# Attention outputs with features on partitions, summed over three groups with weights spread by DMA

## The chip, the cores and the metric

One core of one Trainium2 chip runs the whole step. The metric is device microseconds of that core, as the median of several executions. Its engines are TensorE (PE, matmuls, with its weight loads shown apart as PEld), VectorE (DVE), ScalarE (ACT), GpSimd (POOL) and SyncE (SP), which here issues most of the DMA transfers. Each engine runs its own list of instructions in order; a wait on another engine holds up all that stands behind it in the same list.

## The reference, cut to what matters

The kernel is one step of a decoder for 1024 prompt tokens and 64 sample tokens of width 1024. It has a projection to queries, keys, values and gates, causal pooling as a second branch, dilated attention in three groups of four heads of 64 features, gates, an output projection and an MLP. The groups have reach and stride (128, 1), (512, 4) and (2048, 16). Over 1024 tokens the third group's keys of one residue all fit one block. Each group gives values and the log of its softmax sum, and the groups are mixed with a softmax over these:

```python
def masked_softmax_stats(s, valid):
    s = jnp.where(valid, s, -jnp.inf)
    m = jnp.max(s, axis=-1, keepdims=True)
    p = jnp.exp(s - m)
    den = jnp.sum(p, axis=-1, keepdims=True)
    return p / den, (m + jnp.log(den))[..., 0]

def combine_groups(outs, lses, dtype):
    wts = jax.nn.softmax(jnp.stack(lses, axis=0), axis=0)
    o = jnp.einsum('gbth,gbthd->bthd', wts, jnp.stack(outs, axis=0))
    B, T = o.shape[:2]
    return o.reshape(B, T, ATTN_OUT_WIDTH).astype(dtype)

    branch_b = jnp.einsum('btc,cd->btd', attn, w_pb)
```

## The kernel before

All large products are matmuls over operands that are split into two parts (a rounded one and the rest), with three products summed. Weights come by DMA in panels into one of three places and are split there by ACT (line 108) and DVE (line 109). The stretch from 60 to 166 us makes the third group's queries, keys and values (g2) and its attention, 166 to 300 the second's (g1), 300 to 396 the first's (g0); to 472 us come the gates and the end of the attention, then dense products to the end.

Prompt tokens are in eight blocks of 128 per group. A block's projection is a gemm over 24 matmuls for each of q, k and v (tiles pq, pk, pqk, pv). Between two gemms, and in the middle of each, the kernel calls `step()`, which lets every running generator go on to its next `yield`. So a `yield` in the attention's code is one place further in PE's list, about one gemm or half a gemm, and PE's list is the order of the program text. The order on DVE, ACT and POOL is set by a scheduler, not by the text; each engine then runs its list in order. `behind_pe` ties an instruction to the place of PE's list where it was written. `soon` puts it off to the next step.

For each block `attention()` (from line 574) makes the scores (tile sg, line 586, two halves of the rows), masks them (line 595, a DVE operation that also gives the statistics st), takes exponentials (line 596, ACT), transposes the probabilities on PE (tile tp, line 605), copies them out (pT, line 608), and multiplies them with the values (tile po, line 617): the transposed probabilities are the stationary operand, 128 columns, and the 64 features of a head move, so that the result has tokens on partitions and features along the row. With two key blocks there are 16 such products per block, with one there are 8. ACT copies the result to oc (line 620), and DVE puts the statistics beside it (line 621).

For g2 and g1 oc is stored in DRAM (o_d, lines 694 and 697). For g0 it stays; the other groups' oc of the same 128 tokens are loaded (olg0b, lines 687 and 688), the statistics are gathered (md, lines 700 and 701), `weights()` (lines 625 to 636) forms the softmax over the groups by eight small operations (last one line 635), and `weigh()` (lines 638 to 643) multiplies and adds on DVE. Three steps later (five for the last block) two transposes per block (tile tc, line 709) turn the sum to features on partitions, ACT copies it out (line 651), and it is stored to attn_d (line 656). `branches()` (from line 1009) loads it back as raw_b, with the pooling branch, and splits it into the operand ab of the product pb (and pa). The gate's products (pga, pgb) run meanwhile; line 998 on DVE and line 999 on ACT follow each.

The copies of the new keys for the cache are made in kw (line 917, two buffers) and stored.

## Time and profile before

| | |
|---|---|
| median of 3 runs | 1532.62 us (1532.09 to 1534.24) |
| the profiled execution's own time | 1536.69 us |
| its span | 1534.8 us |
| granted clock, mean | 0.997 |
| PE busy | 1519.1 us (99%) |
| DVE busy | 880.0 us (57%) |
| ACT busy | 519.1 us (34%) |
| POOL busy | 204.3 us (13%) |
| PE's share of the chain that ended last | 89% |

The page is of one execution. Busy time of an engine is the union of its instructions; a matmul's own duration holds a tail that overlaps the next one's, so the pace of a group of matmuls is read from its start to the start of what follows. Rows of groups give line, engine, operation, the tiles out<-in, shapes, count, busy time and mean ns of one, and the idle time ahead of them with what ended most of it. Rows in order of time give start, duration and the same names, with an idle time in brackets. The granted clock is a share of full speed.

### The profile page before, as it was taken

The page shows a single profiled execution, that of the slowest core. Times are in us where ns is not written, and L with a number is a line of the kernel's source. Part 1 is how long each engine was busy: PE and PEld are TensorE (multiplying, and loading weights), DVE is VectorE, ACT ScalarE, POOL GpSimd, SP SyncE. Part 2 cuts the span into 40 slices and gives each one's busy share as a digit, 9 for nine tenths or more (in the row PEclk, how much of TensorE's full clock was granted, in tenths as well). Part 3 has the DMA queues.
Part 4 walks back from the last instruction along what each step waited for, and adds up shares of the span by engine and source line. Part 5 has one row for each costly group of instructions (what it writes and reads, how often), then busy time and mean ns, then how long its engine had stood idle before and what let it go on. Part 6 is the DMA issues. An engine that isn't in the chain of part 4 may idle for free.

```text
span 1534.8 us, 25518 instructions
## 1 busy us (share of the span) xinstructions
PE 1519.1 (99%) x9785; PEld 1474.7 (96%) x9785; DVE 880.0 (57%) x1948; ACT 519.1 (34%) x1613; POOL 204.3 (13%) x245
## 2 busy tenths in 40 slices
PE   9999999999899999999999999999999999999998
PEld 8989888889899999999999999999999999999998
DVE  7655656678755434344575565555555556655556
ACT  8567755677753222222331111111111211112100
POOL 1611256256200000010000000000000000000000
PEclk9999999999999999999999999999999999999999
DMA  5312678655455353584131331322312223222102
GB/s 200 104 50 87 190 168 201 184 138 135 128 147 186 127 180 109 165 264 168 64 107 54 107 104 57 107 69 91 107 63 97 92 72 110 70 95 100 35 8 117
DMA packets 104535, 178.65 MB, mean 116 GB/s; under 512 B 16919, under 2 KB 69725, under 8 KB 103198
## 3 DMA queue, kind: packets, MB, share of 16 engines
q1 hardware_dynamic: 98302, 126.70, 27.4%
q0 software_dynamic: 6112, 50.33, 9.7%
q8 instruction: 77, 1.26, 0.3%
q14 instruction: 44, 0.36, 0.1%
HBM read 155.54 MB, written 65.10 MB: 144 GB/s over the span
## 4 chain that ended last, share of the span: by engine, by line
PE 89%; DMA 3%; DVE 3%; ACT 2%; POOL 1%; issue 1%; SPq 0%; DVEq 0%; ACTq 0%; POOLq 0%
PE py L147 25%; PE pz L147 24%; PE pgb L147 6%; PE ph L147 6%; PE pqk L147 5%; PE pga L147 5%; PE pv L147 3%; PE pa L147 3%; PE a L261 3%; PE pb L147 2%; DMA raw_qkv<-in_w_in_dram 1%; PE pq L147 1%; PE pk L147 1%; PE pog1b L617 1%; DMA olg0b<-o_d 1%
## 5 line engine op out<-in xcount | busy, mean ns | idle before, releaser
L147 PE MATMUL pz<-act,places 128*128 128x384 f32 (+1 forms) x2304 | 382.4, 326 | 0.0
L147 PE MATMUL py<-z,places 128*128 128x384 f32 (+1 forms) x2304 | 381.5, 327 | 0.0
L147 PEld LDWEIGHTS pz<-act,places 128*128 128x128 f32 x2304 | 379.5, 188 | 0.4
L147 PEld LDWEIGHTS py<-z,places 128*128 128x128 f32 x2304 | 379.5, 188 | 0.0
L1194 DVE TENSOR_TENSOR y<-y,py 128x384 f32<-128x384 f32 (+1 forms) x360 | 188.2, 530 | 112.7 <-PE py L147 112.3
L1176 ACT ACTIVATE z<-r 128x384 fp32r<-128x384 f32 (+1 forms) x96 | 48.7, 508 | 323.9 <-DVE r L1175 323.9
L1175 DVE SCALAR_TENSOR_TENSOR r<-pz,rbh 128x384 f32<-128x384 f32 (+1 forms) x96 | 51.2, 534 | 173.2 <-PE pz L147 173.2
L1205 POOL DMA_DIRECT2D out_kv_sample_dram<-in_cache_kv_dram x44 | 21.8, 495 | 934.7 <-ACT places L108 913.1
L108 ACT ACTIVATE places<-raw_u 128x512 fp32r<-128x512 f32 x64 | 38.4, 627 | 266.7 <-PE py L147 259.9
L147 PE MATMUL pga<-act,places 128*128 128x384 f32 (+1 forms) x576 | 99.0, 330 | 0.0
L147 PE MATMUL pgb<-act,places 128*128 128x384 f32 (+1 forms) x576 | 97.8, 326 | 0.0
L147 PE MATMUL ph<-act,places 128*128 128x384 f32 (+1 forms) x576 | 95.9, 327 | 0.0
L147 PEld LDWEIGHTS pga<-act,places 128*128 128x128 f32 x576 | 95.6, 190 | 0.3
L147 PEld LDWEIGHTS pgb<-act,places 128*128 128x128 f32 x576 | 95.4, 188 | 0.0
L147 PEld LDWEIGHTS ph<-act,places 128*128 128x128 f32 x576 | 94.8, 188 | 0.3
L550 POOL TENSOR_TENSOR mr<-ms,mhalf 128x4 f32<-128x4 f32 (+2 forms) x39 | 51.3, 1317 | 109.1 <-DVE ms L549 103.9
L147 PE MATMUL pqk<-places,act 128*128 128x512 f32 x240 | 60.7, 402 | 0.0
L1178 DVE TENSOR_TENSOR z<-q,z 128x384 fp32r<-128x384 f32 (+1 forms) x96 | 51.3, 535 | 8.1
L109 DVE TENSOR_TENSOR places<-raw_d,places 128x512 fp32r<-128x512 f32 x64 | 41.4, 689 | 23.2 <-ACT places L108 23.2
L147 PEld LDWEIGHTS pqk<-places,act 128*128 128x128 f32 x240 | 44.5, 191 | 9.8 <-issue 0.2
L757 POOL TENSOR_TENSOR pcv<-pcv,sc 128x256 f32<-128x256 f32 x64 | 47.6, 772 | 42.6 <-DMA pcv<-in_cache_kv_dram 16.0
L1177 DVE TENSOR_TENSOR q<-r 128x384 f32<-128x384 f32 (+1 forms) x96 | 51.2, 535 | 2.7
(296 smaller groups left out, 2040.8 us busy)
## 6 DMA issues: line engine op xcount, KB each, us to landing
out_kv_sample_dram<-in_cache_kv_dram POOLq DMA_DIRECT2D x36, 960.0 KB, 5.6
raw_u<-in_w_up_dram SPq DMA_DIRECT2D x64, 256.0 KB
raw_d<-in_w_down_dram SPq DMA_DIRECT2D x64, 256.0 KB
raw_qkv<-in_w_in_dram SPq DMA_DIRECT2D x36, 256.0 KB
pck<-in_cache_kv_dram SPq DMA_DIRECT2D x32, 256.0 KB
pcv<-in_cache_kv_dram SPq DMA_DIRECT2D x32, 256.0 KB
out_kv_sample_dram<-in_cache_kv_dram POOLq DMA_DIRECT2D x8, 1008.0 KB, 5.4
kts<-in_kT_dram SPq DMA_DIRECT2D x20, 256.0 KB
```

Of the source, the lines that this page charges most:

```text
L108: ins = s_.activation(dst_hi, src, AF.Copy)
L109: v_.tensor_tensor(dst_lo, src, dst_hi.bitcast(F32), op=ALU.subtract)
L147: last_mm[0] = t_.matmul(out, lhs(a, k), rhs(b, k), start=(j == 0), stop=(j == len(terms) - 1))
L261: last_mm[0] = t_.matmul(pts[m][:, :n], wt[:, a, kk, m * P:(m + 1) * P], act4[b][kk][:, :, part4(c)], start=(p == 0 and kk == 0), stop=(p ...
L550: g_.tensor_tensor(r[:n, :H], ms[:n, :H], mhalf[:n, :H], op=ALU.pow)
L757: behind_pe(g_.tensor_tensor(tv, tv, sc[:, j + n, :].unsqueeze(2).to_broadcast([P, 4, HD]), op=ALU.mult))
L1175: v_.scalar_tensor_tensor(r[:, :n], pzs[m][:, :n], 0.0, rbh[:, c0:c0 + n], op0=ALU.max, op1=ALU.mult)
L1176: s_.activation(z[:, m, 0, :n], r[:, :n], AF.Square)
L1177: v_.tensor_tensor(q[:, :n], r[:, :n], r[:, :n], op=ALU.mult)
L1178: v_.tensor_tensor(z[:, m, 1, :n], q[:, :n], z[:, m, 0, :n].bitcast(F32), op=ALU.subtract)
L1194: v_.tensor_tensor(yc, yc, py[:, :n], op=ALU.add)
L1205: ins = g_.dma_start(d, a)
```

## The change

The product of probabilities and values is turned round: the values, 64 columns of a head, are the stationary operand and the transposed probabilities (128 tokens) move. The result has features on partitions, a head on the lower 64 and the next on the upper 64, so the array is used in two column halves; neighbouring products go to different halves. Their number is the same. Here are the products of one block of the third group on PE (tile po), with what follows them, before:

```order
L617 MATMUL pog2b_1547<-v_2_1068,pTg2b_0_1471 128x64 x2
L617 MATMUL pog2b_1547<-v_2_1068,pTg2b_1_1499 128x64 x2
L440 MATMUL pl_1_1555<-ext_429,lin 128x384
L570 MATMUL tqg2b_1559<-cst,qk_4_1336 128x128 x4
L147 MATMUL pv_5_1567<-places,act_74 128x256 x16
```

And the last two of the four after, with the same followers:

```order
L626 MATMUL pog2b_1546<-pTg2b_0_1471,v_2_1075 64x128
L626 MATMUL pog2b_1546<-pTg2b_1_1499,v_2_1075 64x128
L444 MATMUL pl_1_1553<-ext_434,lin 128x384
L579 MATMUL tqg2b_1557<-cst,qk_4_1339 128x128 x4
L147 MATMUL pv_5_1565<-places,act_74 128x256 x16
```

Before, two products of one half of the probabilities (pT ..._0) run, then two of the other (pT ..._1), each 128 partitions by 64. After, the output is 64 partitions by 128 and the halves alternate, twice pT ..._0 and pT ..._1.

Two blocks now share one tile oc of 512 columns. The results of g2 and g1 are stored by pairs in an order by features (o_d), the statistics stay in tiles (sta) and go through DRAM once per group (st_d) into md, which is there before g0 starts. g2's blocks are taken in another order (`res8`), with the same strides.

For g0 `weights()` lays its result out as 12 columns; one transpose per block (tile tw, line 751), one step behind `weights()`, gives 12 rows of 128; DVE copies them (wT, line 755), a pair's are stored (w_d, line 758), and `combine()` loads each row spread over 64 partitions (ww and w2) and the other groups' values (o1, o2), and multiplies and adds whole pairs (lines 695, 696, 697, 705 and 706). The transposes tc and the copies behind them are gone; attn_d is stored once per pair (line 708). PE around the weights of block 3, before, where the sum was transposed (tile tc, the operand oc is the finished sum):

```order
L147 MATMUL pv_7_5359<-places,nat_02_5165 128x256 x4
L147 MATMUL pv_7_5359<-places,nat_04_5167 128x256 x4
L147 MATMUL pv_7_5359<-places,nat_06_5169 128x256 x4
L709 MATMUL tcg0b_5389<-cst,ocg0b_5109 128x128 x2
L605 MATMUL tpg0b_0_5411<-cst,smg0b_0_5273 128x128 x4
L147 MATMUL pga_0_0_5448<-act_74,places 128x384 x8
```

And after (tile tw, the operand cw is the weights):

```order
L147 MATMUL pq_7_5135<-places,nat_02_5089 128x256 x4
L147 MATMUL pq_7_5135<-places,nat_04_5091 128x256 x4
L147 MATMUL pq_7_5135<-places,nat_06_5093 128x256 x4
L751 MATMUL twg0b_5173<-cst,cwg0b_5109 12x128
L615 MATMUL tpg0b_1_5176<-cst,smg0b_1_4966 128x128 x4
L596 MATMUL sg0b_0_5183<-qkTg0b_4796,qkTg0b_5036 128x128
```

The transpose of block 3 has moved from behind pv_7 to behind pq_7, two gemms earlier, and it waits for the weights rather than for the sum. DVE's list after, up to the copy behind that transpose (ce, cm and cw are the weights' tiles, ms_7_0 the mean squares of the queries of block 7, raw_ga a panel of the gates):

```order
L109 TENSOR_TENSOR places<-raw_ga_0_5341,places 128x512
L109 TENSOR_TENSOR places<-raw_ga_512_5345,places 128x512
L650 TENSOR_TENSOR cwg0b_5109<-ceg0b_5108,md 128x12
L809 TENSOR_TENSOR pcv_5047<-pcv_5047 128x512
L109 TENSOR_TENSOR places<-raw_ga_1024_5349,places 128x512
L558 TENSOR_SCALAR ms_7_0_5160<-ms_7_0_5160,xeps_68 128x4
L651 TENSOR_REDUCE cmg0b_5107<-cwg0b_5109 128x4
L810 TENSOR_TENSOR ss<-ss,pcv_5047 128x512
L652 RECIPROCAL cmg0b_5107<-cmg0b_5107 128x4
L654 TENSOR_TENSOR cwg0b_5109<-ceg0b_5108,cmg0b_5107 128x6x2
L913 TENSOR_REDUCE sfm<-osm 128x4
L755 COPY wTg0b_4942<-twg0b_5173 12x128
```

The weights of block 3 end in the row of line 654; three splits of raw_ga and the mean squares of block 7 stand ahead of it.

SP issues in `combine()` the loads of the spread weights and values. The line of kw now has one buffer, and the probabilities' pT two, not three. The diff, cut to its core:

```diff
     dp = pool("dram", space=DRAM)
-    o_d = [None, [dp.tile([512, 264], F32, name=f"o_d1_{h}") for h in range(2)], dp.tile([SEQ, 264], F32, name="o_d2")]
+
+
+    o_d = [None] + [dp.tile([P, 4, 2, R4 - 16], F32, name=f"o_d{g}") for g in (1, 2)]
+    st_d = [None] + [dp.tile([SEQ, 8], F32, name=f"st_d{g}") for g in (1, 2)]
+    w_d = [dp.tile([12, 2 * P], F32, name=f"w_d{u}") for u in range(4)]
...
-        st = rr(ap, [P, 8], F32, name=f"st{name}", tag="st", bufs=6)
+    def attention(g, b, keys, qT, name):
+
+
+        st = md[:, b, 0, :] if g == 0 else sta[g][:, res8(b), :]
...
-            pT = rr(ap, [P, 4, P], F32, name=f"pT{name}_{e}", tag="pT", bufs=3)
+            pT = rr(ap, [P, 4, P], F32, name=f"pT{name}_{e}", tag="pT", bufs=2)
             pTs.append(pT)
             s_.copy(pT[:, :2 * nk, :], tp[:, :2 * nk, :])
...
-        if ahead:
-            ahead()
-        po = short(f"po{name}")[:, :256]
-        for e in range(2):
-            for hp in range(2):
-                h = 2 * hp + e
-                for j, (_, vr) in enumerate(keys):
-                    t_.matmul(po[:, h * HD:(h + 1) * HD], pTs[e][:, hp * nk + j, :], vr[:, h * HD:(h + 1) * HD],
+        po = short(f"po{name}")[:, :256].rearrange("p (j t) -> p j t", j=2)
+
+        for hp in range(2):
+            for j, (_, vr) in enumerate(keys):
+                for e in range(2):
+                    h = 2 * hp + e
+                    t_.matmul(po[e * HD:(e + 1) * HD, hp, :], vr[:, h * HD:(h + 1) * HD], pTs[e][:, hp * nk + j, :],
                               start=(j == 0), stop=(j == nk - 1))
-        out = rr(ap, [P, 264], F32, name=f"oc{name}", tag="oc", bufs=2)
-        s_.copy(out[:, :256], po)
-        v_.tensor_copy(out[:, 256:], st)
-        return out
+        if b % 2 == 0:
+            pair[g] = rr(ap, [P, 512], F32, name=f"oc{name}", tag="oc", bufs=2)
+        dst = pair[g].rearrange("p (j t) -> p j t", j=2)
+        if g == 2:
+            s_.copy(dst[:, :, b % 2::2], po)
+        elif g == 1:
+            s_.copy(dst[:, :, b % 2 * P:(b % 2 + 1) * P], po)
+        else:
+            s_.copy(dst.rearrange("p j (q l) -> p j q l", q=4)[:, :, :, b % 2 * 32:(b % 2 + 1) * 32],
+                    po.rearrange("p j (l q) -> p j q l", q=4))
+
+    sta = [None] + [ap.tile([P, 8, 8], F32, name=f"sta{g}") for g in (1, 2)]
+    pair = {}
 
     def weights(nm, den, name):
 
         mm = rr(ap2, [P, 4], F32, name=f"cm{name}", tag="cm", bufs=2)
...
-        v_.tensor_reduce(mm, nm.rearrange("p g h -> p h g"), axis=AX.X, op=ALU.min)
+        behind_pe(v_.tensor_reduce(mm, nm.rearrange("p g h -> p h g"), axis=AX.X, op=ALU.min))
...
-        v_.tensor_tensor(e, e, mm.unsqueeze(1).to_broadcast([P, 3, 4]), op=ALU.mult)
-        return e
+        w = w.rearrange("p g h -> p (g h)")
+        v_.tensor_tensor(w.rearrange("p (x g y) -> p g y x", x=2, g=3), e.rearrange("p g (y x) -> p g y x", x=2),
+                         mm.rearrange("p (y x) -> p y x", x=2).unsqueeze(1).to_broadcast([P, 3, 2, 2]), op=ALU.mult)
+        return w
 
...
+    def combine(u, oc):
+        byq = lambda t: t.rearrange("p (j l q) -> p j q l", j=2, q=4)
+        tokens = slice(64 * u, 64 * u + 64)
+        def values(g, t):
+            dma(t.rearrange("p (x l) -> p x l", l=64), o_d[g][:, :, :, tokens].rearrange("p q j l -> p (q j) l"))
+            return t.rearrange("p (q j l) -> p j q l", q=4, j=2)
+        def scales(g, t):
+            for x in range(2):
+                behind_pe(dma(t[x * HD:(x + 1) * HD],
+                              bass.AP(tensor=w_d[u].tensor, offset=w_d[u].offset + (6 * x + 2 * g) * 2 * P,
+                                      ap=[[0, HD], [1, t.shape[1]]])))
+        acc = oc.rearrange("p (j q l) -> p j q l", j=2, q=4)
+        o1 = values(1, rr(ap2, [P, 512], F32, name=f"o1_{u}", tag="ow", bufs=1))
+        if u == 3:
+            o2 = values(2, rr(ap1, [P, 512], F32, name=f"o2_{u}", tag="qk", bufs=2))
+        yield
+        yield
+        ww = ap0.tile([P, 1024], F32, name=f"ww{u}", tag="smp")
+        scales(0, ww)
+        if u == 3:
+            w2 = rr(ap1, [P, 512], F32, name=f"w2_{u}", tag="qk", bufs=2)
+            scales(2, w2)
+        yield
+        yield
+        behind_pe(v_.tensor_tensor(acc, acc, byq(ww[:, :512]), op=ALU.mult))
+        v_.tensor_tensor(o1, o1, byq(ww[:, 512:]), op=ALU.mult)
+        v_.tensor_tensor(acc, acc, o1, op=ALU.add)
+        if u < 3:
+            yield
+            o2 = values(2, rr(ap2, [P, 512], F32, name=f"o2_{u}", tag="ow", bufs=1))
+            w2 = ww[:, :512]
+            scales(2, w2)
+            yield
+            yield
+        behind_pe(v_.tensor_tensor(o2, o2, byq(w2), op=ALU.mult))
+        v_.tensor_tensor(acc, acc, o2, op=ALU.add)
+        yield
+        behind_pe(dma_st(attn_d[:, :, :, tokens].rearrange("p j q l -> p (j q) l"), oc.rearrange("p (x l) -> p x l", l=64)))
...
-        oc = yield from attention(g, ([kept[g, b - 1]] if older else []) + [kept[g, b]], qkT, name,
-                                  None if g else others)
-        yield
-        if g == 2:
-            behind_pe(dma_st(o_d[2].rearrange("(l r) c -> r l c", r=8)[b], oc))
+        yield from attention(g, b, ([kept[g, b - 1]] if older else []) + [kept[g, b]], qkT, name)
+        oc = pair[g]
+        yield
+        if g:
+            if b % 2:
+                behind_pe(dma_st(o_d[g][:, b // 2].rearrange("p j l -> p (j l)"), oc))
+            if b == 7:
+                if g == 2:
+                    src, dst = sta[2].rearrange("p r c -> p (r c)"), st_d[2].rearrange("(l r) c -> l (r c)", r=8)
+                else:
+                    src, dst = sta[1].rearrange("p (x q) c -> p x (q c)", x=2), st_d[1].rearrange("(x l q) c -> l x (q c)", x=2, q=4)
+                behind_pe(dma_st(dst, src))
+                yield
+                yield
+                behind_pe(dma(md[:, :, g, :], st_d[g].rearrange("(b p) c -> p b c", p=P)))
+                done.add((g, "max"))
             return
-        if g == 1:
-            behind_pe(dma_st(o_d[1][b % 2].rearrange("(l r) c -> r l c", r=4)[b // 2], oc))
-            return
-        md = rr(ap2, [P, 3, 8], F32, name=f"md{name}", tag="md", bufs=2)
-        behind_pe(v_.tensor_copy(md[:, 0, :], oc[:, 256:]))
-        behind_pe(v_.tensor_copy(md[:, 1:, :], ol[:, :, 256:]))
-        e = weights(md[:, :, :4], md[:, :, 4:], name)
-        o3 = [x[:, :256].rearrange("p (h d) -> p h d", h=4) for x in (oc, ol[:, 0, :], ol[:, 1, :])]
-        weigh(o3, e)
-        for _ in range(5 if b == 7 else 3):
-            yield
-        tp = short4(f"tc{name}")
-        for j in range(2):
-            t_.transpose(tp[:, j, :], oc[:, j * P:(j + 1) * P], ident)
-        store_attn(tp[:, :2, :], P, t0, name)
+        assert {(1, "max"), (2, "max")} <= done
+        w = weights(md[:, b, :, :4], md[:, b, :, 4:], name)
+        yield
+        tp = short(f"tw{name}")[:12, :P]
+        t_.transpose(tp, w, ident)
+        if b % 2 == 0:
+            pair["w"] = rr(ap2, [12, 2 * P], F32, name=f"wT{name}", tag="wT", bufs=1)
+        wT = pair["w"]
+        v_.tensor_copy(wT[:, b % 2 * P:(b % 2 + 1) * P], tp)
+        if b % 2:
+            yield
+            behind_pe(dma_st(w_d[b // 2], wT))
+            yield from combine(b // 2, oc)
...
-            kw = rr(ap, [P, 256], F32, name=f"kw{g}_{b}", tag="kw", bufs=2)
+            kw = rr(ap, [P, 256], F32, name=f"kw{g}_{b}", tag="kw", bufs=1)
```

More of the change, by code (lines that the diff above doesn't have):

```diff
@@ L496, in block_cols, with res8 @@
             return act4[s][k][:, blk // 2, blk % 2 * P:(blk % 2 + 1) * P]
-        return act4[s][k][:, blk % 4, blk // 4:2 * P:2]
+        return act4[s][k][:, blk // 2, blk % 2:2 * P:2]
+    def res8(blk):
+        return blk // 2 + 4 * (blk % 2)
     nat = {}
@@ L573, in transposed @@
         v_.tensor_copy(dst[:, 2:, :n], tp[:, 2:, :n])
-    def attention(g, keys, qT, name, ahead=None):
-        st = rr(ap, [P, 8], F32, name=f"st{name}", tag="st", bufs=6)
+    def attention(g, b, keys, qT, name):
+        st = md[:, b, 0, :] if g == 0 else sta[g][:, res8(b), :]
         nk = len(keys)
@@ L643, in weigh @@
         v_.tensor_tensor(oc[0], oc[0], oc[2], op=ALU.add)
-    def store_attn(tp, n, t0, name):
-        w, h = n // 4, t0 // P % 2
-        if not h:
-            at[0] = rr(ap2, [P, 8, 64], F32, name=f"at{name}", tag="at", bufs=1)
-        s_.copy(at[0][:, :, h * w:(h + 1) * w].rearrange("p (j q) l -> p j q l", j=2),
-                tp.rearrange("p j (l q) -> p j q l", q=4))
-        if h or n < P:
-            end = t0 // 4 + w
-            src = at[0][:, :, :(h + 1) * w]
-            soon(lambda: behind_pe(dma_st(attn_d[:, :, :, end - src.shape[2]:end].rearrange("p j q l -> p (j q) l"), src)))
```

24 lines of the change are left out of this document (10 added, 14 removed).

## The prediction

> **What bounds the kernel now.** First the page: the busy shares of the engines and the chain that ended last.
>
> ```profile
> PE 1519.1 (99%) x9785; PEld 1474.7 (96%) x9785; DVE 880.0 (57%) x1948; ACT 519.1 (34%) x1613; POOL 204.3 (13%) x245
> PE 89%; DMA 3%; DVE 3%; ACT 2%; POOL 1%; issue 1%; SPq 0%; DVEq 0%; ACTq 0%; POOLq 0%
> ```
>
> TensorE (PE) is the bound: any microsecond taken from its stream shortens the kernel, and any wait put into it lengthens it. Next the stretches, since the change touches only the attention (columns: length, then busy time and count of PE, its weight loads, DVE, ACT and POOL, the granted clock, the DMA share and GB/s).
>
> ```profile
> 300.00:396.00 96.00, 92.79 (x727) 80.36 (x727) 72.14 (x214) 68.97 (x298) 56.58 (x68) 1.00 0.57 144
> 396.00:472.00 76.00, 74.24 (x488) 72.69 (x487) 43.81 (x130) 45.05 (x91) 3.38 (x6) 0.98 0.48 144
> 472.00:1534.00 1062.00, 1057.73 (x6434) 1056.41 (x6432) 572.80 (x1098) 203.00 (x377) 29.63 (x52) 1.00 0.31 103
> ```
>
> Group 0's blocks, with the sum over the groups, lie in 300 to 440. There DVE is 75% busy and runs in order, so a chain of small DVE operations is slow there; the last 1062 us are not touched. Last, what PE waited for:
>
> ```profile
> PE tcg0b L709 <- DVE ocg0b L643: 3.0, 2, 2.5
> PE sg1b L586 <- ACT ocg1b L620: 1.4, 1, 1.4
> PE tpg0b L605 <- ACT ocg0b L620: 1.3, 1, 1.3
> PE pv L530 <- DVE places L109: 0.8, 1, 0.8
> ```
>
> PE is hardly ever late, because the transposes of the finished sum (tc) stand three steps of the schedule behind the weights that they need.
>
> **The products of probabilities and values.** All 280 change shape.
>
> ```profile
> L617 PE MATMUL pog0b<-v,pTg0b 128*128 128x64 f32 x120 | 14.6, 274 | 0.0
> L617 PE MATMUL pog1b<-v,pTg1b 128*128 128x64 f32 x96 | 12.0, 275 | 0.0
> L617 PE MATMUL pog2b<-v,pTg2b 128*128 128x64 f32 x64 | 8.0, 268 | 0.0
> ```
>
> These busy times hold the tail of each group of records; what a group takes from the stream is read from its start to the next start.
>
> ```profile
> 358.81 0.68 PE L802 MATMUL pss<-kts,qSs 128*32 128x136 f32 x16
> 359.41 2.00 PE L617 MATMUL pog0b<-v,pTg0b 128*128 128x64 f32 x16
> 361.25 0.50 PE L570 MATMUL tqg0b<-cst,qk 128*128 128x128 f32 x3
> 213.03 1.00 PE L617 MATMUL pog1b<-v,pTg1b 128*128 128x64 f32 x8
> 213.86 0.39 PE L570 MATMUL tqg1b<-cst,qk 128*128 128x128 f32 x2
> 340.45 0.49 PE L586 MATMUL sg0b<-qkTg0b,qkTg0b 64*128 64x128 f32 x4
> 341.54 0.50 PE L147 MATMUL pqk<-places,nat 128*128 128x512 f32 x1
> ```
>
> Sixteen records take 1.84 us and eight 0.83, 104 to 115 ns each. A block with two key blocks has 16, one with a single key block 8: 11 groups of 16 and 13 of 8 (176 + 104 = 280 records, as 120 + 96 + 64 above), so 11 x 1.84 + 13 x 0.83 = 31.0 us. The new form loads 64 columns and moves 128, its neighbours in different column halves. No row shows it. The nearest are the scores, in halves by rows with 128 moved (four rows of x4, of which the first is shown; 340.45 to 341.54: 16 in 1.09 us, 68 ns each), and pss, in quarters by columns with 136 moved (358.81 to 359.41: 16 in 0.60 us, 38 ns). At the rate of the scores 280 take 19.0 us, a gain of 12.0; at that of pss 10.6, a gain of 20.4; if halves do not overlap, the 110 ns remain and the gain is 0. I take the scores, two halves as here, less one microsecond for the many groups of 8, whose first record has nothing to overlap with: **-11**. The Trainium skill (TensorE: Matmul & The Clock Gate, Part 3, The mechanism) speaks against it: a weight load overlaps running matmuls only where the row group differs, and here both halves hold all rows. By that rule this term is near 0. The pss rows, all 128 rows in four column groups at 38 ns, speak for overlap among columns.
>
> **The transposes.** Eight pairs (tc) go and eight single ones (tw, 128x12 to 12x128) come.
>
> ```profile
> 379.33 0.38 PE L709 MATMUL tcg0b<-cst,ocg0b 128*128 128x128 f32 x2
> 379.55 0.60 PE L605 MATMUL tpg0b<-cst,smg0b 128*128 128x128 f32 x4
> ```
>
> A pair takes 0.22 us (379.33 to 379.55), one I put at half: 8 x 0.11 = **-0.9**.
>
> **The old waits for tc go.** They are 3.0 us, and the longer one had a price behind it:
>
> ```profile
> 285.50:290.00 4.50, 4.50 (x27) 4.38 (x25) 3.52 (x17) 3.43 (x23) 2.18 (x3) 0.62 0.93 259
> 396.00:400.00 4.00, 4.00 (x20) 3.86 (x18) 1.33 (x4) 1.68 (x6) 2.17 (x4) 0.67 0.27 71
> 410.00:414.00 4.00, 4.00 (x40) 3.78 (x38) 2.25 (x12) 3.73 (x9) 0.00 (x0) 1.00 0.24 81
> 285.72 4.63 PE L147 MATMUL pk<-places,nat 128*128 128x256 f32 x24
> 384.47 3.13 PE L147 MATMUL pk<-places,nat 128*128 128x256 f32 x24
> ```
>
> After the 1.4 us wait of sg1b the granted clock is 0.62 and 24 matmuls take 4.63 us, not 3.13: 1.5 us lost. After the 2.5 us wait of tc it is 0.67. After the 1.3 us wait of tpg0b it stays 1.00. So a wait over about 1.4 us costs some 1.5 us more, and removing tc gives 3.0 + 1.5: **-4.5**. The 1.3 us stay, as that wait is for the copy out of the products, which remains. On the clock the Trainium skill (the same page, Part 1, What's actually happening) has it fall after an idle window of some 3.4 us; by that the new waits below would cost no clock, and the sum would be 4.5 us lower. The row of 0.62 behind 1.4 us of waiting differs, and I go by the row.
>
> **New waits: tw.** It stands one step behind the weights, not three. PE is in order: the other half's P transposes, the next scores and the next projection are queued behind it, and DVE's masks wait for those scores. I set PE's time at the place of tw (the start of what follows it there) against the end of the weights (L635 before):
>
> ```profile
> 339.92 0.60 PE L605 MATMUL tpg0b<-cst,smg0b 128*128 128x128 f32 x4
> 341.60 0.17 DVE L635 TENSOR_TENSOR ceg0b<-ceg0b,cmg0b 128x12 f32<-128x12 f32 x1
> 354.24 0.60 PE L605 MATMUL tpg0b<-cst,smg0b 128*128 128x128 f32 x4
> 355.02 0.17 DVE L635 TENSOR_TENSOR ceg0b<-ceg0b,cmg0b 128x12 f32<-128x12 f32 x1
> 368.31 0.60 PE L605 MATMUL tpg0b<-cst,smg0b 128*128 128x128 f32 x4
> 370.72 0.15 DVE L635 TENSOR_TENSOR ceg0b<-ceg0b,cmg0b 128x12 f32<-128x12 f32 x1
> 382.85 0.60 PE L605 MATMUL tpg0b<-cst,smg0b 128*128 128x128 f32 x4
> 390.30 0.16 DVE L635 TENSOR_TENSOR ceg0b<-ceg0b,cmg0b 128x12 f32<-128x12 f32 x1
> 412.34 0.60 PE L605 MATMUL tpg0b<-cst,smg0b 128*128 128x128 f32 x4
> 414.11 0.17 DVE L635 TENSOR_TENSOR ceg0b<-ceg0b,cmg0b 128x12 f32<-128x12 f32 x1
> ```
>
> Late by these: block 0 1.8 us, block 1 1.0, block 2 2.6, block 3 7.6, block 5 1.9. DVE sheds the copies of statistics ahead of them (two or three of about 0.2 us each), so I take 1.2, 0.7 and 1.9 for the first three. In block 3 the new DVE order has the mean squares of pq_7 and three splits of raw_ga ahead of the last weights operation; those need pq_7's end, just before tw, the ACT squares and splits, so 4.7 to 6.3, taken as 5.0. In block 5 the gate's product sga_0_1, which needs all of pga_0_1, stands ahead of L650; tw is right behind pga_0_1: at least 0.55 for it (the row of 405.21 below) and 4 x 0.18 for the rest, with a split and two operations on pairs before them; I take 3.0 (1.3 to 5). Blocks 4, 6 and 7 have no old row at their place; by the same DVE operations I take 2.0, 1.0 and 1.7 (0.5 to 2.5 each); the product sga_2_0 stands ahead of block 7's weights as in block 5. Sum: 1.2 + 0.7 + 1.9 + 5.0 + 2.0 + 3.0 + 1.0 + 1.7 = **+16.5** (10 to 24 by the ends). At least three exceed 1.4 us: 3 x 1.5 = **+4.5** (0 to 7) for the clock.
>
> **Transfers.** SP issues eight value loads of 256 KB in place of 16 of 132, and newly the weights, spread over 64 partitions (3 MB in all). DVE's products wait for them in its queue ahead of the next block's masks. Before, only a copy waited for such a load:
>
> ```profile
> L701 DVE COPY mdg0b<-olg0b 128x16 f32<-128x16 f32 x8 | 1.4, 176 | 5.5 <-DMA olg0b<-o_d 5.5
> 405.21 0.55 DVE L998 TENSOR_TENSOR sga<-pga,rb_g 128x384 f32<-128x384 f32 x1
> 439.26 0.42 DVE L643 TENSOR_TENSOR ocg0b<-ocg0b,olg0b 128x256 f32<-128x256 f32 x1
> 472.10 2.24 PE L147 MATMUL pa<-ab,places 128*128 128x384 f32 x12
> ```
>
> These 5.5 us in eight blocks show in no wait of PE but the two for tc. The loads of the spread weights stand two steps behind the weights' store and the first products two more; a step is about a gemm of 24 matmuls (3.13 us, the row of 384.47), so some 12 us cover a store and a load. If that cover is gone, the next block's masks are late, then its exponentials and P transposes on PE; I take 0 (0 to 9, three waits of 3 us). At the end 32 us lie between the last sum (439.7) and pa (472.1), most of it the loads and splits of ab; **+0.5** (0 to 4). One buffer of kw, not two, holds back raw_qkv's issues behind a store once, where the pv of the second group already waited for its panel: **+1** (0 to 3). The DVE products are as many elements as before and ACT's eight copies (off the path) cost nothing.
>
> **Sum.** -11 - 0.9 - 4.5 + 16.5 + 4.5 + 0.5 + 1 = +6.1. The profiled execution took 1536.69 us, so 1542.8 in its frame; it lies 4.07 above the median of the runs, which has its clock and its waits, so 1532.62 + 6.1 = **1538.7**. By the bounds of the waits alone (10 to 24) it runs from 1532 to 1546.
>
> **Rivals.** *The weights are in time.* DVE loses 24 copies of statistics and 16 of md, and the weights come earlier: block 0 to 3 0.6, 0.1, 1.3, 3.0, then 1.4, 1.4, 0.4 and 1.1, 9.3 in all, and one fall of the clock, with kw's wait at 0: -11 - 0.9 - 4.5 + 9.3 + 1.5 + 0.5 = -5.1, 1527.5. For it: DVE is only 58% busy from 396 on. Against: DVE is in order, and its new order keeps foreign work ahead of the last operation. It decides once the waits of tw and the clock behind them stay under 13 us.
> *They cancel.* The waits are 12.5 with one fall of the clock: -11 - 0.9 - 4.5 + 12.5 + 1.5 + 1 = -1.4, 1531.
> *The halves do not overlap*: then 110 ns a record stay, 6.1 + 11 = +17.1, 1549.7. The pss rows speak against.
> *The spread weights are late*: three products hold up masks, and these PE, 3 us each: +15, 1548. For it: four dependent transfers per pair; against, the 12 us of cover.
>
> **Chances.** Tw's waits win (slower) 0.42, own range 1532 to 1546; weights in time (faster) 0.28; cancel 0.14; late spread weights 0.10; halves serial 0.06. A measurement of this kernel tells about 0.2%, 3 us, from no change. That gives faster 0.28, same 0.14, slower 0.58. The range 1522 to 1549 leaves out the far ends of the first rival (a gain of pss's size among them) and of the serial halves.
>
> **What would show it.** Records of po at 60 to 70 ns: the first term; 110: serial. Waits of twg0b on DVE in the table of waits, 9 to 21 us in all with block 3 the longest, and a granted clock near 0.65 behind the longer ones: the loss. No tw waits, or under 9 us: the first rival. Waits of DVE on ww or w2 with PE idle behind them: the late transfers. A fall that comes from the stretch behind 472 us would make all of this wrong.

## The result and the profile after

The changed kernel takes 1568.02 us (median of 4, 1567.06 to 1568.71); the kernel before takes 1532.66 beside it. The ratio is 1.0229, with a 95% interval of 1.0211 to 1.0246: 35 us slower. The direction was the one forecast. The size was not: 6 us were forecast, and 1568 lies far above the stated range of 1522 to 1549.

The profiled execution of the changed kernel took 1567.48 us with a span of 1565.7, so the two spans differ by 30.9 us. The other 4.5 us come from the executions that were profiled: the one before lay 4.07 us above its median, the one after 0.54 below its own. The last experiment returns to it.

First the table of waits of the kernel after, for PE (us in total, times, the longest).

```profile
PE twg0b L751 <- DVE cwg0b L654: 23.2, 8, 6.2
PE tpg0b L615 <- ACT ocg0b L636: 5.5, 2, 3.1
PE pa L147 <- ACT places L108: 3.6, 2, 3.0
PE pv L539 <- DVE places L109: 0.7, 1, 0.7
```

All eight tw wait. Two further waits, of tpg0b and pa, were not in the forecast's sum. The stretches after, in the columns of those shown of before:

```profile
300.00:396.00 96.00, 84.59 (x652) 71.26 (x651) 61.32 (x181) 62.84 (x270) 54.16 (x64) 0.93 0.56 134
396.00:472.00 76.00, 58.74 (x385) 54.20 (x384) 36.37 (x97) 34.74 (x83) 4.97 (x6) 0.87 0.46 119
472.00:1565.00 1093.00, 1085.03 (x6579) 1082.90 (x6577) 588.82 (x1128) 216.87 (x402) 30.11 (x53) 1.00 0.32 105
404.00:412.00 8.00, 3.43 (x22) 2.70 (x22) 1.55 (x8) 0.96 (x2) 0.00 (x0) 0.69 0.89 234
```

PE is idle for 11 us between 300 and 396 and for 17 us between 396 and 472, where it had been idle for 3 and 2. The granted clock in these is 0.93 and 0.87, from 1.00 and 0.98; where two waits follow each other (404 to 412) its mean is 0.69. Narrower windows show that it does not sink a little: it is 0.50 in six stretches of 6.8 us each (from 366.1, 386.6, 407.1, 424.2, 441.2 and 499.3) and 1.00 between them. The kernel before has three such stretches, of 3.4 us each (from 176.8, 286.0 and 395.2). Then the rows in order of time, for PE, with idle time in brackets:

```profile
389.58 0.37 PE L751 MATMUL twg0b<-cst,cwg0b 128*12 128x128 f32 x1 [6.16 <-DVE cwg0b L654]
396.11 1.09 PE L626 MATMUL pog0b<-pTg0b,v 128*64 128x128 f32 x16
397.14 0.66 PE L579 MATMUL tqg0b<-cst,qk 128*128 128x128 f32 x4
405.45 0.27 PE L751 MATMUL twg0b<-cst,cwg0b 128*12 128x128 f32 x1 [2.25 <-DVE cwg0b L654]
408.84 1.12 PE L615 MATMUL tpg0b<-cst,smg0b 128*128 128x128 f32 x4 [3.12 <-ACT ocg0b L636]
426.15 0.37 PE L751 MATMUL twg0b<-cst,cwg0b 128*12 128x128 f32 x1 [4.31 <-DVE cwg0b L654]
499.10 0.88 PE L147 MATMUL pa<-ab,places 128*128 128x384 f32 x2 [3.02 <-ACT places L108]
```

Block 3's tw waits longest, 6.16 us. The products (396.11 to 397.14) take 1.03 us for 16 records, where they took up to 1.84. A product leaves two records, so these 16 are the eight products of a block with two key blocks.

To see where the 30.9 us are, PE's rows are laid end to end from the first pq of the attention (61.20 before, 62.02 after) to the second group of pa (475.22 and 505.83): a group's stream time is from its start to the next start, without the idle time ahead of that.

| from the first pq to the second pa, us | before | after | difference |
|---|---|---|---|
| idle | 8.3 | 36.8 | +28.6 |
| products of probabilities and values (280 records) | 30.7 | 19.5 | -11.2 |
| transposes tc, tw | 2.0 | 1.4 | -0.6 |
| all other work of PE (same work, lower clock) | 373.1 | 386.1 | +13.0 |
| sum | 414.0 | 443.8 | +29.8 |

From there to the end both streams agree within 0.3 us; 0.8 us lie ahead of the first pq. In the row of other work the largest parts are the first group's scores (+3.7), pa and pb (+3.1), the gate's products pga (+2.7) and the transposes tp (+1.9): all stand right behind waits, in the stretches at half clock.

So the gain in the products came as reckoned. What took it away is 29 us of new waits and 13 us of slower clock. The longest waits are for tw. Whether tw is the whole cause had to be tried, since a wait that is removed can uncover another.

### The profile page after: what moved, and what is told of

It is laid out like the page before. It is cut to its first block, busy times and chain, and to the rows that moved or that the text cites. A ratio compares the mean times of both kernels' runs of the same rounds, so it can differ in the third digit from the quotient of the medians.

```text
span 1565.7 us, 25449 instructions
## 1 busy us (share of the span) xinstructions
PE 1520.1 (97%) x9777; PEld 1464.2 (94%) x9777; DVE 875.6 (56%) x1896; ACT 517.4 (33%) x1605; POOL 202.6 (13%) x245
## 4 chain that ended last, share of the span: by engine, by line
PE 85%; DMA 5%; DVE 4%; ACT 2%; issue 1%; POOL 1%; SPq 1%; DVEq 0%; POOLq 0%; ACTq 0%
PE py L147 24%; PE pz L147 24%; PE ph L147 6%; PE pgb L147 5%; PE pqk L147 5%; PE pga L147 4%; PE pa L147 3%; PE a L265 3%; PE pv L147 3%; PE pb L147 2%; DMA raw_qkv<-in_w_in_dram 1%; PE pk L147 1%; DMA ww<-w_d 1%; PE sg0b L596 1%; PE pq L147 1%
## 5 line engine op out<-in xcount | busy, mean ns | idle before, releaser
L147 PE MATMUL pa<-ab,places 128*128 128x384 f32 (+1 forms) x288 | 53.7, 335 | 3.6 <-ACT places L108 3.6
L147 PEld LDWEIGHTS pa<-ab,places 128*128 128x128 f32 x288 | 49.5, 194 | 4.4 <-ACT places L108 4.4
```

What stands on the lines that cost most here:

```text
L147: last_mm[0] = t_.matmul(out, lhs(a, k), rhs(b, k), start=(j == 0), stop=(j == len(terms) - 1))
```

## The experiments

Theories at the start: the wait theory has the loss in tw's place, too close behind the weights; the spread theory has it in the road of the weights through DRAM, which blocks DVE and keeps the tile oc taken.

**Tw without its wait.** The transposes read a constant; the groups' sum then has wrong weights.

```diff
-        t_.transpose(tp, w, ident)
+        t_.transpose(tp, ident[:, :12], ident)
```

> The changed kernel, with the eight transposes tw reading twelve columns of the constant identity instead of the weights (so the groups' sum uses wrong weights); everything else stays, tw included, but tw no longer waits for DVE. Wait theory (PE's loss is that tw stands too soon behind the weights: 23.2 us of waits in the changed kernel's profile, and the lower clock behind them): the time falls from 1568 by 28 to 40 us, to 1528 to 1540. Spread theory (the loss is that the spread weights come back late, so that DVE and the shared tile oc hold PE up; tw's wait is only where this shows first): the time stays above 1555, the waits of tpg0b for the copy to oc grow well beyond 5.5 us.

Measured: 1557.51 us, ratio 1.0170 (1.0154 to 1.0186). Some 10 us come back. The table of waits of PE, and the longest in order of time:

```profile
PE tpg0b L615 <- ACT ocg0b L636: 14.0, 2, 8.9
PE pa L147 <- ACT places L108: 5.3, 2, 5.0
399.14 1.12 PE L615 MATMUL tpg0b<-cst,smg0b 128*128 128x128 f32 x4 [8.94 <-ACT ocg0b L636]
```

The 23.2 us are gone, and the wait of tpg0b for the copy to oc has grown from 5.5 to 14.0. That is far from the wait theory's 1528 to 1540. The two signs of the spread theory are there (over 1555, and waits for oc well beyond 5.5), but 10 us of gain say that tw's wait is more than the place where the other shows first. There are two waits, and part of the second was hidden by the first. What the copy waits for stands on ACT in the kernel after; a row of DVE follows:

```profile
408.41 0.37 ACT L636 COPY ocg0b<-pog0b 128x256 f32<-128x256 f32 x1 [5.02 <-DMA attn_d<-ocg0b]
412.83 1.09 DVE L696 TENSOR_TENSOR o<-o,ww 128x512 f32<-128x512 f32 x1 [6.79 <-DMA ww<-w_d]
```

The tile oc has two buffers, each now a pair of blocks. The third pair's first copy (408.41) waits until the first pair's sum has been stored to attn_d. PE waits for the copy itself: it empties the place in PSUM that the next transposes of probabilities take (the row of 408.84 above, right behind the copy's end). How long that road is: from tw of block 1 (350.71) to the store of the first pair's sum, issued at 404.85, 54 us go by. DVE's wait for the spread weights (6.79 us) belongs to the next pair's road; in all DVE waits for them five times, 19.3 us.

**The wait alone, in the kernel before.** Eight transposes of the weights, unused, where tw stands.

```diff
         weigh(o3, e)
-        for _ in range(5 if b == 7 else 3):
+        yield
+        t_.transpose(short(f"tw{name}")[:12, :P], e.rearrange("p g h -> p (g h)"), ident)
+        for _ in range(4 if b == 7 else 2):
             yield
```

> The kernel before, with eight transposes of the weights added one step behind them, as the changed kernel has tw; their result is not read, and the old transposes tc keep their place. Products, sums and transfers are those of before. Wait theory: the wait alone costs most of the loss, so 1548 to 1565 us, with 12 to 25 us of PE waiting for the weights on DVE and a lower clock behind. Spread theory: the wait alone is short, under 8 us in all, and the time under 1542.

Measured: 1550.75 us, ratio 1.0142 (1.0111 to 1.0173), 19 us slower than the kernel before.

```profile
PE twg0b L706 <- DVE ceg0b L635: 16.8, 8, 4.0
```

The wait by itself, with old layout and old sum, makes 16.8 us of idle PE and about 19 of time, within what the wait theory said. The sum lies next to the forecast's 16.5, in part by luck: by block the waits are 2.2, 1.2, 2.5, 4.0, 0.8, 1.4, 2.3 and 2.4, and the forecast is off by up to 1.6 us in both directions. The clock pays little here: it is 0.50 in three stretches of 3.4 us, and the other work of PE, laid end to end as above, takes 373.7 us, against 373.1 in the first profile of the kernel before and 370.7 in the second (last experiment). In the changed kernel the order on DVE makes the waits 23.2.

**The halves one after the other.**

```diff
-        for hp in range(2):
-            for j, (_, vr) in enumerate(keys):
-                for e in range(2):
+        for e in range(2):
+            for hp in range(2):
+                for j, (_, vr) in enumerate(keys):
```

> The changed kernel, with the products of probabilities and values ordered by column half (all of the one half, then all of the other) instead of alternating. If neighbours in different column halves overlap, sixteen products take about 1.8 us instead of 1.03, and the kernel gets 5 to 12 us slower (less than 280 x 50 ns, as PE's waits for the weights take some of it up). If the gain comes from the 64-column stationary operand alone, the pace stays and the time is within 2 us of the changed kernel.

Measured: 1569.92 us, ratio 1.0255 (1.0236 to 1.0273); against the changed kernel's 1.0229 the intervals touch, so a cost of 2 to 4 us is likely and not certain.

```profile
344.21 1.58 PE L626 MATMUL pog0b<-pTg0b,v 128*64 128x128 f32 x16
345.72 0.65 PE L579 MATMUL tqg0b<-cst,qk 128*128 128x128 f32 x4
```

Sixteen records take 1.51 us (94 ns each), not 1.03 and not 1.8; groups of eight take 0.59 to 0.60 in both orders. So the gain has two halves. With the halves one after the other the products cost 24.7 us in all, 6.0 less than before (115 to 94 ns in groups of 16, 104 to 74 in groups of 8): that comes with the 64-column stationary operand. The alternation gives the other 5.2, and only in groups of 16 (94 to 64 ns). So the pace is neither of the two that were expected. The profiled execution, which took 1574.00 us, is 5.5 us longer than the changed kernel's from the first pq to the second pa; the medians show 2 of it.

**Weights formed earlier.** They need the statistics only, which the change gathers ahead (md), so they can follow the block's exponentials.

```diff
@@ attention, behind the exponentials and two steps
+        if g == 0 and {(1, "max"), (2, "max")} <= done:
+            kept["w", b] = weights(md[:, b, :, :4], md[:, b, :, 4:], name)
@@ attend_rest
-        w = weights(md[:, b, :, :4], md[:, b, :, 4:], name)
+        w = kept.get(("w", b))
         yield
```

> The changed kernel with the weights of a block formed three steps earlier, right behind its exponentials (they need only the statistics, not the block's sum); tw, the store, the spread loads and the products keep their places. Wait theory: PE's waits for tw vanish or nearly so and the time falls to 1525 to 1540; spread theory: the spread loads come no earlier relative to the products' places, DVE still waits for them, oc stays taken, and the time stays above 1555.

Measured: 1558.34 us, ratio 1.0174 (1.0157 to 1.0190). As with the constant, tw no longer waits and oc takes over:

```profile
PE tpg0b L617 <- ACT ocg0b L638: 13.5, 2, 8.4
```

The wait theory falls here for the second time. The spread theory's bound of 1555 holds in both, but it had a wait for tw alone under 8 us and a time under 1542, and these were 16.8 and 1550.75. So neither is the whole. A third was put: two waits in series that hide each other.

**The shorter road alone.** Five steps fewer between tw and the store of the sum.

```diff
-            yield
             behind_pe(dma_st(w_d[b // 2], wT))
@@ combine
-        yield
         yield
         ww = ap0.tile(...)
...
         if u < 3:
-            yield
             o2 = values(2, ...)
             scales(2, w2)
-            yield
             yield
...
         v_.tensor_tensor(acc, acc, o2, op=ALU.add)
-        yield
         behind_pe(dma_st(attn_d[...], ...))
```

> The changed kernel with the road from tw to the stored sum made five steps shorter: the weights' store directly behind the copy of tw, the spread loads one step behind it, the third group's loads directly behind the first sums and their product one step later, the store of the sum directly behind the last sum; tw keeps its place. Series theory, formed after the first runs: two waits of PE hide each other, tw's for the weights (23.2 us) and tpg0b's for the copy to oc, which waits until the sum of two pairs ago has gone (5.5 us, but 13.5 to 14.0 when tw's is taken away); each alone gives back only part. Then here the waits for oc go and those for tw stay: 1555 to 1564 us. If the road to the store is the cause alone, it falls below 1545; if tw alone is, it stays at 1566 to 1570.

Measured: 1558.60 us, ratio 1.0165 (1.0139 to 1.0190).

```profile
PE twg0b L747 <- DVE cwg0b L654: 26.3, 8, 7.5
```

No wait of tpg0b for oc is left in the table of PE, and that of pa for places is gone (one of 1.1 us for another operation of DVE stands there); those of tw stay and grow a little. Early weights alone return 9.7 us, the shorter road alone 9.4.

**Both, and tw earlier too.** The early weights with the short road; then tw one step earlier; then two steps earlier, ahead of the block's products; then the last pair's products a step closer to their loads. The edits beyond the two above:

```diff
@@ tw one step earlier
         w = kept.get(("w", b))
-        yield
         tp = short(f"tw{name}")[:12, :P]
@@ two steps earlier: in attention(), tw and the copy wT as turned()
+        if g == 0 and ("w", b) in kept:
+            turned(b, kept["w", b], name)
         po = short(f"po{name}")[:, :256].rearrange("p (j t) -> p j t", j=2)
@@ the last products closer
             scales(2, w2)
         yield
-        yield
+        if u < 3:
+            yield
```

> Both at once: the weights of a block formed three steps earlier and the shorter road to the stored sum. Series theory: PE waits for neither, and the time falls well below either alone (1558 with the early weights), to 1525 to 1540, near or under the kernel before (1531.7). If the two do not lie in series and something else holds PE up (the spread loads themselves, the slower clock for another reason), it stays above 1548.

> As the one with both, and tw itself one step earlier too, so that the sum of a pair is stored six steps earlier than in the changed kernel. Series theory: 1522 to 1538, not slower than with both, unless tw's earlier place meets late weights again. Where the end of the attention (3.6 us of waits of pa and the clock behind them) is what is left, this one shortens it by one step.

> As the one with early weights, tw one step earlier and the shorter road (1538.8 us), with tw another step earlier, ahead of the block's products, so the last sum is stored a step earlier as well. If what is left there is the end of the attention (pa's waits of 2.5 us and the clock behind them) and the waits for oc (1.4 us), it falls by 2 to 6 us, to 1533 to 1537. If tw meets late weights again (it now stands two steps behind them), PE waits for it by 3 us or more and the time rises over 1541.

> As the one before it, and the last pair's products one step behind their spread loads instead of two. If pa still waits for the splits that come behind the last sum, it gains 1 to 4 us more; if the loads take that step to land, DVE waits for ww instead and nothing changes (within 2 us).

| kernel | median, us | ratio to before (95%) |
|---|---|---|
| changed | 1568.02 | 1.0229 (1.0211 to 1.0246) |
| early weights | 1558.34 | 1.0174 (1.0157 to 1.0190) |
| shorter road | 1558.60 | 1.0165 (1.0139 to 1.0190) |
| both | 1549.36 | 1.0104 (1.0087 to 1.0121) |
| both, tw one step earlier | 1538.78 | 1.0038 (1.0023 to 1.0053) |
| both, tw two steps earlier | 1534.78 | 1.0016 (1.0000 to 1.0032) |
| the same, last products closer | 1536.44 | 1.0023 (1.0011 to 1.0034) |

With the early weights and the short road the time was to fall to 1525 to 1540, and it is 1549.36: the series theory missed there. The gains just add, 9.7 and 9.4 alone and 18.7 together; that the waits hide each other shows in the tables of waits, and not in the time. The waits of PE with both, and two rows of DVE in order of time:

```profile
PE pa L147 <- ACT places L108: 4.8, 1, 4.8
PE sg0b L596 <- ACT pTg0b L620: 3.6, 1, 3.6
PE sg0b L596 <- DVE pTs L871: 3.6, 1, 3.6
361.98 1.08 DVE L697 TENSOR_TENSOR o<-o,ww 128x512 f32<-128x512 f32 x1 [3.21 <-DMA ww<-w_d]
400.46 1.07 DVE L697 TENSOR_TENSOR o<-o,ww 128x512 f32<-128x512 f32 x1 [4.18 <-DMA ww<-w_d]
```

DVE stands still for the spread weights ahead of each of PE's two waits for a place of the scores: the shorter road has the products closer to their loads. That one leads to the other is not shown. In all DVE waits for ww 21.7 us here, 13.0 with tw one step earlier and 6.9 with two; but with tw one step earlier the first of these waits is longer (4.96 us), and no wait of PE follows. With tw one step earlier the two waits of PE are gone and the time falls by 10.6 us, to 1538.78, just above the range expected; with two steps it falls by 4 more, inside its range. In that best one the attention's clock is back:

```profile
300.00:396.00 96.00, 90.04 (x719) 74.32 (x716) 64.86 (x196) 66.81 (x294) 56.83 (x69) 1.00 0.62 150
396.00:472.00 76.00, 72.68 (x484) 69.92 (x483) 45.40 (x109) 40.20 (x82) 1.75 (x3) 0.98 0.56 166
PE sg1b L596 <- ACT ocg1b L638: 2.3, 1, 2.3
PE sft L940 <- DVE sres L935: 1.9, 1, 1.9
PE pga L147 <- ACT places L108: 1.9, 1, 1.9
```

It takes back 33 of the 35 us, and its products are as cheap as the changed kernel's (19.5 us). It is level with the kernel before, within 0.2%, and no version tried beats that: PE's small waits from the first pq to the second pa, none over 2.3 us, sum to 15.8 against 8.4 in the last profile of the kernel before, and its other work takes 374.9 against 370.7, which together take the whole gain of 11. The two buffers of pT and the one of kw, which all these versions have, were not tried apart. The last variant was to gain 1 to 4 us or nothing; it gained nothing.

**Tw where tc stood.** The changed kernel with tw two steps later and the road's first two parts a step shorter each.

```diff
         w = weights(md[:, b, :, :4], md[:, b, :, 4:], name)
-        yield
+        for _ in range(3):
+            yield
...
         if b % 2:
-            yield
             behind_pe(dma_st(w_d[b // 2], wT))
@@ combine
-        yield
         yield
         ww = ap0.tile(...)
```

> The changed kernel with tw two steps later, where the old transposes tc stood, and the weights' store and the spread loads one step closer behind it each, so that the sums keep their places. Series theory: PE's waits for tw go (under 3 us in all), those for the copy to oc grow to 9 to 15 us as they did with the constant tw (14.0) and the early weights (13.5), and the time falls by 8 to 14 us, to 1554 to 1560. If tw's place alone were the cause, it would fall to 1525 to 1540.

Measured: 1548.40 us, ratio 1.0102 (1.0076 to 1.0128).

```profile
PE tpg0b L615 <- ACT ocg0b L636: 15.3, 3, 8.5
PE pa L147 <- ACT places L108: 5.4, 1, 5.4
```

Tw's waits are gone and oc's are 15.3 us, at the upper end of what was expected. The time is 6 us below the expected range, and 8 above the range for tw's place alone: 20 us come back, twice as much as with the constant, though the waits for oc are as long. Laid end to end, PE's idle time is 25.4 us here and 30.1 with the constant, its other work 379.0 and 383.5. With the constant, still one step behind the weights, the scores wait twice 2.0 us for places in PSUM that DVE empties late, one of them tw's own; here such waits are 0.3 us. So tw's place one step behind the weights seems to cost more than its wait for them; how these 10 us divide was not tried. The wait for oc remains, and the shorter road, which removes it, shows that it is a cause of its own.

**Dummy work in the waits, for the clock.**

```diff
+        for _ in range((14, 4, 22, 50, 18, 36, 20, 20)[b]):
+            t_.transpose(tp, ident, ident)
         t_.transpose(tp, w, ident)
```

> The changed kernel with dummy transposes of the identity put in front of each tw, as many as fill most of that wait at 0.11 us each (14, 4, 22, 50, 18, 36, 20 and 20; 184 in all); they write the tile that tw then overwrites. The waits stay as long as they are for DVE, but PE works through them. If the lower clock behind the waits costs what the changed kernel's trace shows (scores, gates and transposes of the first group at 0.6 to 0.7 of full speed, some 12 us), the time falls by 6 to 13 us, to 1555 to 1562. If the clock costs only the 4.5 us of my sum or less, it falls by under 5 us; if the dummies cost more than they save, it rises.

Measured: 1563.28 us, ratio 1.0198 (1.0182 to 1.0214). The first row gives its span and clock, the next its wait for tw:

```profile
core 0: 1559.0 us, clock 0.996
PE twg0b L754 <- DVE cwg0b L654: 4.5, 6, 1.9
```

The mean clock rises from 0.986 to 0.996, and the median falls by 4.7 us, less than the 6 to 13 that the slowed rows promised; the intervals of the two ratios touch (1.0211 to 1.0246 and 1.0182 to 1.0214). The trace says where the rest went. From the first pq to the second pa the same other work takes 376.3 us in place of 386.1, so filling these waits gives 9.8 us of clock back. PE's idle time falls by 17.2 us, but tw and the dummies take 23.0 in place of 1.4: they cost 4.4 us more than the waits that they fill. (In blocks 3 and 4 no wait was left behind them.) That gives 5.5 us in this execution.

**The kernel before, once more.**

> The kernel before, profiled once more. My sum counted 4.5 us for two old waits of tc on DVE (3.0 us) and the clock behind the longer one, from an execution that took 1536.69 us against a median of 1532.6. If that wait belongs to the kernel, it is there again with 2 to 3 us and the execution takes about 1536; if it belonged to that one execution, the execution takes 1531 to 1534, the wait is under 0.6 us, and the term should not have stood in a sum against the median.

Measured: 1534.35 us, one execution.

```profile
PE tcg0b L709 <- DVE ocg0b L643: 1.7, 1, 1.7
```

The wait of tc is there, once, with 1.7 us, in place of 3.0. It lies between the two cases put: the wait belongs to the kernel, but its size changes from one execution to the next, and the 4.5 us of the forecast were its price in an execution 4 us above the median. The clock behind it differs, too. Here, in the columns of the other stretches, are those behind the waits of sg1b (1.45 us) and of tc (1.74) in this run, and then, from the changed kernel, those behind tw's wait of block 5 (4.31) and of block 7 (2.64):

```profile
285.10:288.30 3.20, 3.20 (x17) 3.20 (x17) 2.80 (x15) 2.16 (x15) 1.01 (x2) 0.50 1.03 278
394.40:398.00 3.60, 3.10 (x22) 2.70 (x22) 1.43 (x4) 1.56 (x6) 2.01 (x3) 1.00 0.24 74
424.30:430.90 6.60, 4.75 (x29) 4.17 (x30) 4.94 (x22) 4.60 (x8) 0.00 (x0) 0.50 0.47 122
456.00:462.00 6.00, 5.90 (x39) 5.93 (x40) 1.00 (x3) 1.36 (x3) 0.00 (x0) 1.00 0.77 270
```

A wait of 1.45 us has the clock at half behind it, one of 1.74 and one of 2.64 have not. The length of a single wait does not decide it.

## Why the prediction was wrong in size

Between the two profiles, from the first pq to the second pa, PE loses 29.8 us where the sum had 6.1. Of the 23.7 that are missing, 13.6 are idle time and 10.0 the clock. The step that failed in its mechanism is the term "Transfers, 0": it missed a wait altogether. The steps that failed in size are the clock, the waits for tw and the end of the attention.

- **Products, -11.** Right: 30.7 to 19.5 us, -11.2. The rate of the scores (68 ns) was the right neighbour; the new pace is 64 to 74 ns. The reason given, that neighbours in different halves overlap, can stand for 5.2 us of it at most: the other 6.0 come without alternation.
- **Transposes, -0.9.** Right in size: -0.6.
- **Old waits of tc, -4.5.** Too much for a sum against the median: 1.7 us in the second profile, with an execution nearer to the median, and no lower clock behind it.
- **Waits for tw, +16.5 (10 to 24).** Under-sized, in its range: 23.2. By block 1.8, 0.7, 2.8, 6.2, 2.3, 4.3, 2.6 and 2.6 against 1.2, 0.7, 1.9, 5.0, 2.0, 3.0, 1.0 and 1.7. Block 3 is the longest, as said, and so is the order of what stands ahead of it on DVE. Added to the kernel before alone, the wait is 16.8 us.
- **Clock behind them, +4.5.** The largest miss: 13.0 us in the rows of other work, where the sum had 4.5 for the new waits less 1.5 for the old one. 9.8 come back where tw's waits are filled. By the term's own list five waits exceed 1.4 us, not three, which would have made it 7.5. The rule behind the term, some 1.5 us for each wait over 1.4, does not hold: eight waits in the old kernel (16.8 us) came with three stretches of 3.4 us at half clock, the twelve in the changed kernel with six of 6.8, and behind single waits of 1.74 and 2.64 us the clock stayed full. What decides between no fall, 3.4 us and 6.8 us at half clock stays open. The prediction's sum by an idle window of some 3.4 us (the Trainium skill, TensorE: Matmul & The Clock Gate, Part 1, What's actually happening) overlooks its own 5.0 us for block 3; here a fall stands behind a wait of 1.45 us too.
- **Transfers, 0 (0 to 9).** This is the step that failed in its mechanism. I asked only whether DVE's products would hold up the next masks, and named 12 us of cover. The cover was not enough: DVE waits 19.3 us for the spread weights. For the second pair the weights' store was issued at 396.58, the loads at 405.54, and the product began at 412.83. And I had not followed the tile oc: in the kernel before one block's copy is short-lived, now two buffers hold a pair each until its sum has been stored, nine steps and a round trip through DRAM behind tw. That gave 5.5 us of waits of PE in the changed kernel, and 14.0 as soon as tw's went.
- **End of the attention, +0.5 (0 to 4).** Wrong: from the first pgb (23.8 us late) to the second pa (30.6) another 6.8 us are lost, 3.6 of them waiting, the rest at the lower clock. The "32 us of cover" was mostly full of loads and splits of ab, which begin when the attention's last sum is done; with the shorter road alone the wait of pa for places is gone.
- **One buffer of kw, +1.** The pv that waited 0.8 us for its split panel waits 0.7 now: no cost shown there.

Of the rivals, "the spread weights are late" described half of the truth by another way: it had PE held up over the masks by 9 us, and put 0.10 on it as an alternative to tw's waits. Its sign came, DVE waiting on ww, and it came together with tw's waits; PE was held up by the tile oc. The first rival, the weights in time, fell: all eight wait, 23.2 us, far above the 9 named. Serial halves fell as well: 64 ns a record.

The rule of the Trainium skill (TensorE: Matmul & The Clock Gate, Part 3, The mechanism) that would have put the products' gain near 0 did not decide here: 11.2 us were gained. It is not refuted either: it speaks of weight loads that overlap, 6.0 of the 11.2 us come without alternating halves, and groups of 8 keep their pace in either order.

## What to carry to other kernels

When a step moves towards its producer, look first at the engine that runs in order and is the bound: an operation on it that waits for a chain of small operations elsewhere costs more than the operation itself, 16.8 us here for eight transposes of 0.1. When values that were finished in place now make a round trip through DRAM, count for how many steps each buffer on the way stays taken, and who writes it next; part of that wait shows only when the one ahead of it is removed, here 14.0 us in place of 5.5. After each wait that is taken away, read the table of waits again: the early weights gave back 10 us, the shorter road 10, both 19, and both with an earlier tw 33. None of it made the change a gain.

## What was not expected of the hardware

Sixteen records of the new product take 1.03 us with alternating column halves and 1.51 us with one half after the other, but eight take 0.59 to 0.60 in both orders. In the serial order of 16, two products in a row also add to the same place in PSUM, which they do not in the groups of 8; the runs do not part this from an overlap of the halves. And the clock: it was granted in full or at half, and at half for 3.4 us at a time in the kernel before and 6.8 in the changed one. Behind waits that sum to 32 us (tw, oc and pa) the same rows of PE took 13.0 us longer, two fifths of the waits; in the old kernel with tw added, 16.8 us of waits made the same rows at most 3.0 us longer. So in these runs a wait has no fixed price in clock.
